# Gate products over 64 rows and one activation table in a hybrid decoder layer

## The chip, the core and the metric

The kernel runs on one core of one Trainium2 chip. The metric is the time of one execution on the device, in microseconds (us); every time given is that or a stretch of a profiled execution. The engines are TensorE (PE, with its weight loads as PEld), VectorE (DVE), ScalarE (ACT), GpSimd (POOL) and SyncE (SP, which only starts transfers here).

## What is computed

One layer over 1024 tokens and 16 meta tokens set ahead of them, model width 1024. After a norm, one projection gives queries, keys, values, and two streams of width 512, `x_rec` and `y_rec`. Attention runs in a sliding window of 128 with sinks. The other half of the heads is a gated linear recurrence, and this is where the change lies:

```
gate_r = einsum("btnc,ncd->btnd", xb, w_a) + b_a      # 8 blocks of 64 x 64
gate_i = einsum("btnc,ncd->btnd", xb, w_x) + b_x
r, i   = sigmoid(gate_r), sigmoid(gate_i)
log_a  = -8 * r * softplus(-lam)
a      = exp(log_a)
u      = sqrt(-expm1(2 * log_a)) * (i * x)
h[t]   = a[t] * h[t-1] + u[t]                          # along time
rec    = gelu(y_rec) * h
```

Here `x` is `x_rec` after a causal convolution over four steps. Attention and `rec` are joined, multiplied by `w_out` (1024 x 1024), normed and added. Then follow a norm and a feed-forward part of width 4096 with a squared ReLU, normed and added again. All inputs and outputs are float32.

## The kernel before

Every product is made in three parts: each operand is split into a high part, rounded for the matmul, and a low part, the rest. `split` (L93) does it with a cast (ACT unless told otherwise) and a subtraction on DVE; `mm3` (L122) multiplies high by high (L124), high by low (L125) and low by high (L126) into one PSUM bank. The feed-forward part, two thirds of the time, uses sums of blocks to save products; the change does not touch it but for one instruction.

The recurrence works with channels on the 128 partitions, four column groups `c` of 128 channels (two blocks of 64), and 1040 time steps along the free axis.

- `conv` (L606) leaves `xc[c]`. `gh` and `gl` (L691 and L692) hold the gate weights as 128 x 128 matrices, two 64 x 64 blocks on the diagonal and zeros besides; `graw` (L683) is cleared by POOL and filled by four transfers.
- `gates(c)` (L697) splits `xc[c]`, and for each of the two gates and each of three pieces of time (348, 348 and 344 steps) runs one `mm3` over 128 rows into a bank and evicts it with a sigmoid on ACT. Then DVE multiplies the input gate by `xc[c]` (L715).
- `decay(c)` (L719) makes `a` by an exponential and `tanh(-4 r softplus)` (a function in the exponential's table), both on ACT. Since `-expm1(2 log_a) = -tanh(log_a / 2) * (1 + a)^2`, the root of the tangent times `1 + a` is the factor that the reference calls `mult`.
- `recur(c)` (L725) takes the root on ACT (L727 by way of `lut`), then on DVE multiplies by `1 + a` (L728), by the gated input (L729), and scans along time (L730).
- `rec_out(c, half)` (L732) takes the GeLU of `y_rec`, multiplies by `h` on DVE (L736) and splits the product for the output matmul. `half` is rows 0 to 511 or 512 to 1023.
- `load_wo` and `split_wo` (L742 and L749) fetch and split the eight row blocks of `w_out`; `out_mm` (L787) multiplies a tile of 128 tokens by row blocks 0 to 3 (attention) and 4 to 7 (`rec`).

All activations that need a table go through `lut` (L81), which keeps them in program order on ACT. A change from one table to another puts a table load of its own on ACT (ACT_TABLE_LOAD in the profile, at L82).

The order on the engines is not the program's. A scheduler at build time runs through the program on an estimate of the durations, and gives every engine the ready instruction with the first place in the program; `deferred` (L73) sets a piece back by 1000 places, and `behind` (L105) puts an instruction after a given one without a wait. The order that comes out is fixed in the kernel; the chip adds only waits. So the projections of `y_rec` (`next_fill`, L658) are spread between attention and gates, and row blocks 0 to 3 of the output product of the first four token tiles fill PE while the recurrences are made. Tiles share buffers by tag: the split output weights 1 to 7 use tag "a", whose 16 buffers hold the normed input until the last projection is done.

At the very end, `finish_late` (L1235) needs a square root; L1322 takes one of a constant ahead of it, so that its table is there.

Of the kernel before, what the change touches and what calls it, by code (L numbers as in the profile page):

```python
# [37 lines left out]
def hybrid_layer(  # L38
# [42 lines left out]
    def lut(*args, **kwargs):  # L81
        ins = nc.scalar.activation(*args, **kwargs).ins  # L82
        if last_lut[0] is not None:
            tc.add_manual_dep(
                ins, last_lut[0],
                mybir.DependencyInfo(
                    mybir.DependencyClass.NoSync, mybir.DependencyReason.DATA
                ),
                reason="lut",
            )  # L90
        last_lut[0] = ins.name

    def split(hi, lo, src, eng=None):  # L93
        if eng is None:
# [381 lines left out]
    nc.vector.tensor_tensor(acc4, acc4, sv, op=ALU.mult)  # L476
    nc.vector.tensor_scalar(sv, lam, -1.0, 0.0, op0=ALU.mult, op1=ALU.max)
    nc.vector.scalar_tensor_tensor(sv, acc4, 2.0, sv, op0=ALU.mult, op1=ALU.add)
    m8sp = const.tile([P, NLRU], F32, name="m8sp")
    m4sp = const.tile([P, NLRU], F32, name="m4sp")  # L480
    nc.vector.tensor_scalar(m8sp, sv, -8.0, None, op0=ALU.mult)
    nc.vector.tensor_scalar(m4sp, sv, -4.0, None, op0=ALU.mult)


    def put_v(dst, src):
# [194 lines left out]
    attend(*prev)  # L680


    graw = slot("e", [P, 2, NLRU, P])  # L683
    behind(last_pow[0], nc.gpsimd.memset(graw, 0.0).ins)
    for i, w in enumerate((w_a, w_x)):
        for s in range(2):
            r = slice(HD * s, HD * s + HD)
            nc.sync.dma_start(
                graw[r, i, :, r], w[0, s::2].rearrange("n c d -> c n d")
            )  # L690
    gh = slot("e", [P, 2, NLRU, P], F32R)  # L691
    gl = slot("b", [P, 2, NLRU, P], F32R)  # L692
    split(gh, gl, graw)

    rg = [None] * NLRU

    def gates(c):  # L697
        ch, cl = pair("b", [P, TT])
        split(ch, cl, xc[c])
        rg[c] = []  # L700
        for i in range(2):
            t_ = slot("c", [P, TT])
            for t0, n in ((0, 348), (348, 348), (696, 344)):
                flip[0] += 1
                acc = bank(("s", "pt", "o")[flip[0] % 3])
                mm3(
                    acc[:, :n], (gh[:, i, c, :], gl[:, i, c, :]),
                    (ch[:, t0 : t0 + n], cl[:, t0 : t0 + n]), True, True,
                )
                lut(  # L710
                    t_[:, t0 : t0 + n], acc[:, :n], AF.Sigmoid,
                    bias=prm[:, c, 5 + i : 6 + i],
                )
            rg[c].append(t_)
        nc.vector.tensor_tensor(t_, t_, xc[c], op=ALU.mult)  # L715

    av = [None] * NLRU

    def decay(c):  # L719
        r = rg[c][0]  # L720
        av[c] = slot("b", [P, TT])
        lut(av[c], r, AF.Exp, scale=m8sp[:, c : c + 1])
        lut(r, r, AF.Tanh, scale=m4sp[:, c : c + 1])

    def recur(c):  # L725
        r, gi = rg[c]
        lut(r, r, AF.Sqrt, scale=-1.0)  # L727
        nc.vector.scalar_tensor_tensor(r, av[c], 1.0, r, op0=ALU.add, op1=ALU.mult)  # L728
        nc.vector.tensor_tensor(gi, gi, r, op=ALU.mult)  # L729
        nc.vector.tensor_tensor_scan(r, av[c], gi, 0.0, op0=ALU.mult, op1=ALU.add)  # L730

    def rec_out(c, half):  # L732
        o = 512 * half
# [18 lines left out]

    for c in range(NLRU):
        gates(c)
    next_fill()
    for cs in ((0, 1), (2, 3)):
        for c in cs:
            decay(c)
        for c in cs:
            recur(c)  # L760
    load_wo(0, "raw")
    load_wo(1, "raw")
    load_wo(2, "d")
# [529 lines left out]
    for n, (i, q) in enumerate(steps):  # L1293
# [25 lines left out]
            finish_half(q - 1)  # L1319
        if i == 6 and q == 4:  # L1320
            root = small.tile([P, 1], F32, name="root", tag="root")
            lut(root, half_pow, AF.Sqrt, scale=-1.0)  # L1322
    for j in range(4):
        parts = col_parts(6, j)
        for k in finish_late(j, accs[j], parts):
# [33 lines left out]
```

## Time and profile before

| | |
|---|---|
| median of 3 runs | 963.28 us (963.26 to 963.48) |
| profiled execution | 963.19 us, span 960.8 us |
| PE busy | 941.4 us, 4654 matmuls |
| DVE busy | 669.6 us, 945 instructions |
| ACT busy | 501.1 us, 822 instructions |
| POOL busy | 156.7 us, 202 instructions |
| mean granted PE clock | 0.998 of full |

The span is the time from the first to the last instruction of the profiled execution; its own time is a little longer. Busy shares overlap: the engines work side by side. A row of a timeline gives start, duration, engine, source line, operation, output and inputs, and in brackets the idle time before it and what ended it. A row of the windows view gives the stretch, its length, and the busy time of PE, PEld, DVE, ACT and POOL with instruction counts, then the granted clock, the DMA share and GB/s. Rows of groups give count, busy time, mean ns of one, and idle time before. Matmuls are pipelined, so their pace is read from the distance of their starts and not from their durations.

### The profile page before, as it was taken

To read this page: it belongs to the slowest core of one execution; us is meant where nothing else is said; L and a number is where in the kernel's file an instruction comes from. 1 tells how busy PE (TensorE), PEld (TensorE's weight loads), DVE (VectorE), ACT (ScalarE), POOL (GpSimd) and SP (SyncE) were. 2 spreads that over 40 slices of the span, in tenths; PEclk is the share of its full clock that TensorE was granted. 3 is DMA by queue.
4 is the path that set the end of the run, shared out by engine and by line. 5 is a ranking of instruction groups with operands and counts; after the bars stand their busy time and mean duration, and the time that the engine had idled before them with its cause. 6 is when DMAs were issued, how large, how long until landed. Compare 5 with 4: busy or idle time off the path is not lost.

```text
span 960.8 us, 12386 instructions
## 1 busy us (share of the span) xinstructions
PE 941.4 (98%) x4654; PEld 789.1 (82%) x4654; DVE 669.6 (70%) x945; ACT 501.1 (52%) x822; POOL 156.7 (16%) x202
## 2 busy tenths in 40 slices
PE   6999999999999999999999999999999999999997
PEld 6999998888788877888888888788888888888886
DVE  5579989756955796664655465568557776779884
ACT  7556676469634663443555556554433343435441
POOL 4015656600021100000111001100111100003020
PEclk9999999999999999999999999999999999999999
DMA  8111101111235457676546557623667765556422
GB/s 293 46 48 42 39 7 45 41 58 67 87 132 175 150 180 224 192 263 197 197 161 216 163 193 252 213 95 120 171 171 192 194 225 194 180 196 155 110 88 87
DMA packets 85626, 140.74 MB, mean 146 GB/s; under 512 B 5784, under 2 KB 48936, under 8 KB 85568
## 3 DMA queue, kind: packets, MB, share of 16 engines
q1 hardware_dynamic: 75104, 108.51, 34.5%
q0 software_dynamic: 9600, 29.36, 11.7%
q10 hardware_dynamic: 864, 2.10, 0.6%
q8 instruction: 36, 0.59, 0.3%
q14 instruction: 22, 0.18, 0.1%
HBM read 115.70 MB, written 23.07 MB: 144 GB/s over the span
## 4 chain that ended last, share of the span: by engine, by line
PE 88%; issue 5%; ACT 3%; DVE 2%; DMA 1%; POOL 1%; DVEq 0%; SPq 0%; POOLq 0%; ACTq 0%
PE ps_acc L124 11%; PE ps_acc L125 10%; PE ps_acc L126 10%; PE ps_s L126 6%; PE ps_s L125 6%; PE ps_s L124 6%; PE ps_pt L124 6%; PE ps_pt L125 6%; PE ps_pt L126 6%; PE ps_o L124 5%; PE ps_o L126 5%; PE ps_o L125 5%; PE ps_o L585 1%; ACT c L82 1%; PE ps_s L525 1%
## 5 line engine op out<-in xcount | busy, mean ns | idle before, releaser
L95 ACT CAST ws<-raw 128x1024 fp32r<-128x1024 f32 (+1 forms) x70 | 71.8, 1025 | 122.6 <-PE ps_o L125 45.1
L98 DVE TENSOR_TENSOR ws<-raw,ws 128x1024 fp32r<-128x1024 f32 (+1 forms) x71 | 86.3, 1215 | 47.9 <-ACT ws L95 47.8
L124 PE MATMUL ps_acc<-a,ws 128*128 128x256 f32 (+2 forms) x256 | 85.2, 333 | 0.0
L125 PE MATMUL ps_acc<-a,ws 128*128 128x256 f32 (+2 forms) x256 | 84.8, 331 | 0.0
L126 PE MATMUL ps_acc<-a,ws 128*128 128x256 f32 (+2 forms) x256 | 84.8, 332 | 0.0
L98 DVE TENSOR_TENSOR b<-b,b 128x1024 fp32r<-128x1024 f32 (+2 forms) x48 | 57.6, 1200 | 27.0 <-PE ps_o L125 17.4
L95 ACT CAST ws<-e 128x1024 fp32r<-128x1024 f32 x42 | 43.9, 1045 | 60.3 <-PE ps_o L125 26.7
L98 DVE TENSOR_TENSOR ws<-e,ws 128x1024 fp32r<-128x1024 f32 x42 | 51.3, 1222 | 23.0 <-ACT ws L95 23.0
L95 ACT CAST b<-b 128x1024 fp32r<-128x1024 f32 (+2 forms) x48 | 49.5, 1030 | 34.2 <-DVE b L862 33.4
L575 POOL TENSOR_SCALAR_AFFINE_SELECT c<-c 128x512 fp32r<-128x512 f32 x64 | 55.7, 893 | 27.3 <-ACT c L95 15.4
L169 POOL TENSOR_TENSOR rs<-ms,half_pow 128x1 f32<-128x1 f32 (+1 forms) x29 | 21.0, 730 | 211.0 <-DVE ms L165 209.6
L126 PEld LDWEIGHTS ps_acc<-a,ws 128*128 128x128 f32 x256 | 48.2, 188 | 4.9
L124 PEld LDWEIGHTS ps_acc<-a,ws 128*128 128x128 f32 x256 | 48.2, 188 | 4.2
L125 PEld LDWEIGHTS ps_acc<-a,ws 128*128 128x128 f32 x256 | 48.1, 188 | 4.2
L124 PE MATMUL ps_acc<-ws,b 128*128 128x512 f32 (+1 forms) x120 | 46.3, 386 | 0.0
L125 PE MATMUL ps_acc<-ws,b 128*128 128x512 f32 (+1 forms) x120 | 46.0, 384 | 0.0
L126 PE MATMUL ps_acc<-ws,b 128*128 128x512 f32 (+1 forms) x120 | 46.0, 384 | 0.0
L125 PE MATMUL ps_pt<-ws,b 128*128 128x512 f32 x112 | 44.2, 395 | 0.6 <-DVE ws L98 0.6
L126 PE MATMUL ps_pt<-ws,b 128*128 128x512 f32 x112 | 43.9, 392 | 0.0
L124 PE MATMUL ps_pt<-ws,b 128*128 128x512 f32 x112 | 43.9, 394 | 0.0
L124 PE MATMUL ps_s<-ws,b 128*128 128x512 f32 x110 | 43.3, 395 | 0.0
L126 PE MATMUL ps_s<-ws,b 128*128 128x512 f32 x110 | 43.2, 393 | 0.0
(393 smaller groups left out, 2713.4 us busy)
## 6 DMA issues: line engine op xcount, KB each, us to landing
raw<-in_w_ff_dram SPq DMA_DIRECT2D x58, 512.0 KB, 4.3
e<-in_w_ff_dram SPq DMA_DIRECT2D x42, 512.0 KB, 3.9
raw<-in_w_in_dram SPq DMA_DIRECT2D x12, 512.0 KB, 4.9
d<-in_w_ff_dram SPq DMA_DIRECT2D x12, 512.0 KB, 3.8
s_dram<-d POOLq DMA_DIRECT2D x12, 512.0 KB, 3.9
e<-in_w_ff_dram POOLq DMA_DIRECT2D x10, 512.0 KB, 5.4
raw<-in_w_ff_dram POOLq DMA_DIRECT2D x10, 512.0 KB, 5.6
c<-in_x_dram SPq DMA_DIRECT2D x8, 512.0 KB, 8.1
```

The source lines that it names most:

```text
L82: ins = nc.scalar.activation(*args, **kwargs).ins
L95: nc.scalar.copy(hi, src)
L98: low = nc.vector.tensor_tensor(lo, src, f32(hi), op=ALU.subtract).ins
L124: nc.tensor.matmul(dst, lh, rh, start=start, stop=False, skip_group_check=True)
L125: nc.tensor.matmul(dst, lh, rl, start=False, stop=False, skip_group_check=True)
L126: last_mm[0] = nc.tensor.matmul(dst, ll, rh, start=False, stop=stop, skip_group_check=True).ins.name
L169: last_pow[0] = nc.gpsimd.tensor_tensor(rs[:n], ms[:n], half_pow[:n], op=ALU.pow).ins.name
L525: nc.tensor.matmul(dst, q[h][:, c], hi, start=True, stop=False, skip_group_check=True,)
L575: nc.gpsimd.affine_select(out=m[:, :, side, :], in_=f32(m)[:, :, 1, :], pattern=[[0, 4], [-sign, P]], compare_op=op, fill=0.0, base=0, cha ...
L585: nc.tensor.matmul(po[:, :, oc : oc + n], v, m[:, :, pc : pc + n], start=first and k == 0, stop=last and k == 1, skip_group_check=True,)
```

## The change

The gate weights are no longer 128 x 128 matrices with zeros. For each block of 64 input channels, the weights of both gates lie side by side, 64 rows by 128 columns: `gw` is 128 x 4 x 2 x 64. The rows of the upper block hold the input gate first and the recurrence gate second, those of the lower block the other way round. `gates(c)` multiplies the two blocks by matmuls over 64 rows, alternately, into two banks. Each bank then holds both gates of one block of 64 channels, one gate on each half of the partitions. `gbias` holds the biases in that layout, halved.

The sigmoid becomes `(1 + tanh(g/2)) / 2`: the eviction is a tangent with scale 0.5. Two half-partition copies (to `v`) and two half-partition products bring the gates to their channels; the factors one half go into the constants `m4sp` and `m2sp` and the scale of the root. `decay(c - 1)` follows `gates(c)`, `decay(3)` the last filling projection, and the four `recur` come after that, so that all roots stand together. The memset of `graw` is gone. The root of a constant near the end is put behind the last split.

```diff
@@ lut
         last_lut[0] = ins.name
+        return ins
@@ constants
-    m8sp = const.tile([P, NLRU], F32, name="m8sp")
     m4sp = const.tile([P, NLRU], F32, name="m4sp")
-    nc.vector.tensor_scalar(m8sp, sv, -8.0, None, op0=ALU.mult)
+    m2sp = const.tile([P, NLRU], F32, name="m2sp")
     nc.vector.tensor_scalar(m4sp, sv, -4.0, None, op0=ALU.mult)
+    nc.vector.tensor_scalar(m2sp, sv, -2.0, None, op0=ALU.mult)
@@ gate weights
-    graw = slot("e", [P, 2, NLRU, P])
-    behind(last_pow[0], nc.gpsimd.memset(graw, 0.0).ins)
-    for i, w in enumerate((w_a, w_x)):
-        for s in range(2):
-            r = slice(HD * s, HD * s + HD)
+    graw = slot("e", [P, NLRU, 2, HD])
+    for s in range(2):
+        r = HALF[s]
+        for i, w in enumerate((w_x, w_a)):
             nc.sync.dma_start(
-                graw[r, i, :, r], w[0, s::2].rearrange("n c d -> c n d")
-            )
-    gh = slot("e", [P, 2, NLRU, P], F32R)
-    gl = slot("b", [P, 2, NLRU, P], F32R)
-    split(gh, gl, graw)
+                graw[r, :, i ^ s, :], w[0, s::2].rearrange("n c d -> c n d")
+            )
+    gw = [slot("e", [P, NLRU, 2, HD], F32R), slot("b", [P, NLRU, 2, HD], F32R)]
+    split(*gw, graw)
+    gbias = const.tile([P, 2, NLRU], F32, name="gbias")
+    for s in range(2):
+        for i in range(2):
+            nc.vector.tensor_scalar(
+                gbias[HALF[i ^ s], s, :], prm[HALF[s], :, 6 - i], 0.5, None,
+                op0=ALU.mult,
+            )
@@ gates
-        ch, cl = pair("b", [P, TT])
-        split(ch, cl, xc[c])
-        rg[c] = []
-        for i in range(2):
-            t_ = slot("c", [P, TT])
-            for t0, n in ((0, 348), (348, 348), (696, 344)):
+        halves_x = pair("b", [P, TT])
+        split(*halves_x, xc[c])
+        te, to = slot("b", [P, TT]), slot("c", [P, TT])
+        for t0, n in ((0, 348), (348, 348), (696, 344)):
+            accs = []
+            for s in range(2):
                 flip[0] += 1
-                acc = bank(("s", "pt", "o")[flip[0] % 3])
-                mm3(
-                    acc[:, :n], (gh[:, i, c, :], gl[:, i, c, :]),
-                    (ch[:, t0 : t0 + n], cl[:, t0 : t0 + n]), True, True,
+                accs.append(bank(("s", "pt", "o")[flip[0] % 3]))
+            for k, (a, b) in enumerate(((0, 0), (0, 1), (1, 0))):
+                for s in range(2):
+                    nc.tensor.matmul(
+                        accs[s][:, :n], gw[a][HALF[s], c], halves_x[b][HALF[s], t0 : t0 + n],
+                        start=k == 0, stop=k == 2, skip_group_check=True,
+                    )
+            for s, t_ in enumerate((te, to)):
+                lut(
+                    t_[:, t0 : t0 + n], accs[s][:, :n], AF.Tanh, scale=0.5,
+                    bias=gbias[:, s, c : c + 1],
                 )
-                lut(
-                    t_[:, t0 : t0 + n], acc[:, :n], AF.Sigmoid,
-                    bias=prm[:, c, 5 + i : 6 + i],
-                )
-            rg[c].append(t_)
-        nc.vector.tensor_tensor(t_, t_, xc[c], op=ALU.mult)
-
-    av = [None] * NLRU
+        v = slot("c", [P, TT])
+        lo, hi = HALF
+        nc.vector.tensor_copy(v[hi], to[lo])
+        nc.vector.scalar_tensor_tensor(
+            to[lo], te[lo], 1.0, xc[c][lo], op0=ALU.add, op1=ALU.mult
+        )
+        nc.vector.tensor_copy(v[lo], te[hi])
+        nc.vector.scalar_tensor_tensor(
+            to[hi], to[hi], 1.0, xc[c][hi], op0=ALU.add, op1=ALU.mult
+        )
+        rg[c] = v, to, te
@@ decay
-        r = rg[c][0]
-        av[c] = slot("b", [P, TT])
-        lut(av[c], r, AF.Exp, scale=m8sp[:, c : c + 1])
-        lut(r, r, AF.Tanh, scale=m4sp[:, c : c + 1])
+        v, _, te = rg[c]
+        lut(te, v, AF.Exp, scale=m4sp[:, c : c + 1], bias=m4sp[:, c : c + 1])
+        lut(v, v, AF.Tanh, scale=m2sp[:, c : c + 1], bias=m2sp[:, c : c + 1])
@@ recur
-        r, gi = rg[c]
-        lut(r, r, AF.Sqrt, scale=-1.0)
-        nc.vector.scalar_tensor_tensor(r, av[c], 1.0, r, op0=ALU.add, op1=ALU.mult)
+        r, gi, a = rg[c]
+        lut(r, r, AF.Sqrt, scale=-0.25)
+        nc.vector.scalar_tensor_tensor(r, a, 1.0, r, op0=ALU.add, op1=ALU.mult)
         nc.vector.tensor_tensor(gi, gi, r, op=ALU.mult)
-        nc.vector.tensor_tensor_scan(r, av[c], gi, 0.0, op0=ALU.mult, op1=ALU.add)
+        nc.vector.tensor_tensor_scan(r, a, gi, 0.0, op0=ALU.mult, op1=ALU.add)
@@ order
     for c in range(NLRU):
         gates(c)
+        if c:
+            decay(c - 1)
     next_fill()
-    for cs in ((0, 1), (2, 3)):
-        for c in cs:
-            decay(c)
-        for c in cs:
-            recur(c)
+    decay(3)
+    for c in range(NLRU):
+        recur(c)
@@ before the end
-            lut(root, half_pow, AF.Sqrt, scale=-1.0)
+            behind(w_low[0], lut(root, half_pow, AF.Sqrt, scale=-1.0))
```

## The prediction, on record before the change was built

> **What bounds the kernel now.** I read the page first: engine shares and the chain of work that ended last.
>
> ```profile
> span 960.8 us, 12386 instructions
> ...
> PE 941.4 (98%) x4654; PEld 789.1 (82%) x4654; DVE 669.6 (70%) x945; ACT 501.1 (52%) x822; POOL 156.7 (16%) x202
> ...
> PE 88%; issue 5%; ACT 3%; DVE 2%; DMA 1%; POOL 1%; DVEq 0%; SPq 0%; POOLq 0%; ACTq 0%
> ```
>
> The matmul engine is occupied for 98% of the span and makes up 88% of the chain, so a microsecond counts only if matmul time goes away or one of its few gaps closes. The profiled execution took 963.19 us, 2.4 us around a span of 960.8; the median of the three runs is 963.28, 0.09 above it. What the measurement can tell from no change is 0.2%, about 1.9 us.
>
> The edit sits in the gates and what follows them, so the next view is busy time by stretch: gates, the last projection, the output product of the first four row tiles, and two later stretches.
>
> ```profile
> 199.80:219.00 19.20, 19.20 (x107) 17.76 (x106) 6.04 (x6) 12.51 (x26) 0.00 (x0) 1.00 0.17 55
> 219.00:231.30 12.30, 12.30 (x55) 9.99 (x54) 5.57 (x7) 12.15 (x12) 0.00 (x0) 1.00 0.01 1
> 231.30:268.00 36.70, 35.55 (x153) 28.26 (x152) 35.05 (x35) 24.59 (x33) 0.00 (x0) 1.00 0.32 110
> 268.00:340.00 72.00, 72.00 (x347) 59.36 (x346) 46.95 (x71) 36.76 (x90) 11.95 (x24) 1.00 0.45 149
> 340.00:565.00 225.00, 224.32 (x969) 181.13 (x968) 138.18 (x174) 112.70 (x145) 17.57 (x29) 1.00 0.61 198
> ```
>
> After the length of a stretch come PE, PEld, DVE, ACT and POOL busy. PE is full everywhere, even in the gates, where ACT is busy 12.51 of 19.20 and DVE 6.04. The third stretch differs: PE idles 36.70 - 35.55 = 1.15 us and DVE works 35.05 of 36.70. From 268 on PE is full again and DVE at 47 of 72. So what PE wins before 268 should reach the end, and only DVE between 227 and 268 can take it back. The waits of PE between 198 and 270:
>
> ```profile
> PE ps_pt L124 <- ACT a L95: 0.6, 1, 0.6
> PE ps_pt L125 <- DVE ws L98: 0.6, 1, 0.6
> ```
>
> The first is the high half of an output weight, queued on ACT behind the GeLUs; the second is the low half of the first output weight, queued on DVE among the recurrences.
>
> **The change, part by part.**
>
> *Gate products.* Now one column group has two gates x three pieces x three products = 18 matmuls, all over 128 rows, half of them zeros. After it has three pieces x three products x two halves = 18 again, over 64 rows each, all still 348 or 344 columns wide. The count stays at 72. The third group now runs unbroken:
>
> ```profile
> 210.78 0.32 PE L124 MATMUL ps_s<-b,e 128*128 128x348 f32 x1
> ...
> 213.47 0.32 PE L126 MATMUL ps_o<-b,b 128*128 128x344 f32 x1
> 213.63 0.39 PE L124 MATMUL ps_acc<-a,ws 128*128 128x512 f32 x1
> ```
>
> 18 matmuls from 210.78 to 213.63 are 0.158 us each, 72 are 11.4 us. Anything is saved only if the matmuls of the two row halves run side by side; no row of this trace shows 64-row matmuls, so I bound it. Upper end of the cost: no overlap, 11.4 us, nothing saved. Lower end: a pair in the time of one, 36 x 0.158 = 5.7, saving 5.7. Between them stands the weight load, since each matmul keeps its own load of 128 columns:
>
> ```profile
> 60.58 0.28 PE L529 MATMUL ps_s<-km,b 128*128 128x128 f32 x1
> 60.69 0.27 PE L525 MATMUL ps_s<-b,b 128*128 128x128 f32 x1
> 60.80 0.27 PE L529 MATMUL ps_s<-b,b 128*128 128x128 f32 x1
> ```
>
> ```profile
> 60.52 0.19 PEld L529 LDWEIGHTS ps_s<-km,b 128*128 128x128 f32 x1
> ...
> 60.85 0.19 PEld L525 LDWEIGHTS ps_s<-b,b 128*128 128x128 f32 x1
> ```
>
> In the scores, matmuls of only 128 columns still start 0.11 us apart, and so do their loads (0.33 us for three steps). If loads stay one after another, 72 x 0.11 = 7.9 us, saving 3.5. I take this, the nearest row, and keep 0 and 5.7 for the range. The Trainium skill ("TensorE: Matmul & The Clock Gate", Part 3) has matmuls of distinct row groups run together, with a span of one matmul plus about 4 ns per tile; by that a pair costs 0.162 us and 72 save 5.5 us. No row here shows it; it is rival 1.
>
> *Switching the array.* The only matmuls on few rows are the parameter transposes:
>
> ```profile
> 53.38 0.38 PE L286 MATMUL ps_s<-ident,d 128*128 128x128 f32 x2
> 53.69 0.41 PE L439 MATMUL ps_o<-ident,d 8*128 8x8 f32 x4
> 54.03 0.76 PE L497 MATMUL ps_pt<-ident,c 128*128 128x128 f32 x5
> ```
>
> ```profile
> 53.69 0.32 PEld L439 LDWEIGHTS ps_o<-ident,d 8*128 8x128 f32 x4 [0.17 <-issue]
> ```
>
> Their first load starts with the first matmul, not ahead of it, after 0.17 us of load idle. With 0.11 us per full-size transpose the pair at 53.38 should have handed over at 53.60, so about 0.1 us is lost on the way in; I take as much on the way out. The gates come in some five blocks between projection matmuls, ten switches, 1.0 us. If they are cut up by piece (12 blocks, 24 switches at 0.17) it is 4.1, and 0 at best. The Trainium skill ("TensorEngine Tiling (Array Packing)", Key Properties) says that a change of tiling mode drains the array, which speaks against interleaving; the late load at 53.69 agrees with it.
>
> PE: -3.5 + 1.0 = **-2.5 us**.
>
> *ACT.* Rows from 198 to 250:
>
> ```profile
> L82 ACT ACT_TABLE_LOAD x7 | 9.0, 1283 | 0.1
> L82 ACT ACTIVATE c<-c,m4sp 128x1040 f32<-128x1040 f32 x4 | 4.7, 1162 | 0.1
> L82 ACT ACTIVATE b<-c,m8sp 128x1040 f32<-128x1040 f32 x4 | 4.6, 1158 | 0.0
> ...
> L82 ACT ACTIVATE c<-ps_s,prm 128x348 f32<-128x348 f32 x8 | 4.4, 554 | 6.5 <-PE ps_s L126 6.5
> ...
> L82 ACT ACTIVATE c<-c 128x1040 f32<-128x1040 f32 x4 | 4.1, 1065 | 0.0
> ```
>
> ```profile
> 201.26 0.55 ACT L82 ACTIVATE c<-ps_s,prm 128x348 f32<-128x348 f32 x1 [1.20 <-PE ps_s L126]
> ...
> 206.56 0.55 ACT L82 ACTIVATE c<-ps_s,prm 128x348 f32<-128x348 f32 x1 [1.58 <-PE ps_s L126]
> 207.03 0.55 ACT L82 ACTIVATE c<-ps_pt,prm 128x348 f32<-128x348 f32 x1
> ...
> 246.03 1.28 ACT L82 ACT_TABLE_LOAD   x1
> ```
>
> Seven table loads: sigmoid, exponential, square root, exponential, square root, GeLU, and square root again at 246.03 for the final norm. The tangent and exponential rows already share a table. The first, second, fourth and fifth go (one square root load stays), and the one at 246.03 moves to the last FFN steps, where 1.28 us fits into ACT's slack (52% busy over the span). That frees 5 x 1.28 = 6.4 us here; the 24 gate activations, 8 decays and 4 roots keep number and width. The 6.5 us that ACT now waits for gate products can hold three of the four decays. First root, from the first activation at 201.3: 24 x 0.47 + 8 x 1.16 + one split's cast (about 1.0) = 21.6, some 1 us of gaps left, load 1.28, root 1.07: 226.2, against 227.6 now. The ACT-caused PE wait goes: **-0.6 us**. The DVE-caused one I leave in place.
>
> *DVE.*
>
> ```profile
> 222.22 0.69 DVE L640 COPY d<-ps_acc 128x512 f32<-128x512 f32 x1 [1.62 <-PE ps_acc L126]
> 227.66 1.24 DVE L728 SCALAR_TENSOR_TENSOR c<-b,c 128x1040 f32<-128x1040 f32 x1 [4.75 <-ACT c L82]
> 228.82 0.69 DVE L97 CAST ws<-raw 128x1024 fp32r<-128x1024 f32 x1
> ...
> 264.45 1.90 DVE L98 TENSOR_TENSOR b<-d,b 128x512 fp32r<-128x512 f32 x3
> ```
>
> ```profile
> L730 DVE TENSOR_TENSOR_SCAN c<-b,c 128x1040 f32<-128x1040 f32 x4 | 9.3, 2322 | 0.0
> L729 DVE TENSOR_TENSOR c<-c,c 128x1040 f32<-128x1040 f32 x4 | 5.0, 1242 | 0.0
> L728 DVE SCALAR_TENSOR_TENSOR c<-b,c 128x1040 f32<-128x1040 f32 x4 | 4.9, 1235 | 4.8 <-ACT c L82 4.8
> ```
>
> Added per group: two half-partition copies and two half-partition products for the one product of L715 (1.24 us). Width, not partitions, should set their time: 2 x 0.69 (the L97 row) + 2 x 1.24 = 3.9, so +2.6, in all +10.5 us. It lies in 203 to 223, where DVE idles 13.16 of the first stretch's 19.20: free. Without that cover only the last group's copies (2.6 us) would delay its decay. Four bias scalings on 64x4 are noise. From 227.66 to 266.35 DVE runs without a gap, 38.7 us, and PE takes up the last low half about 1 us later:
>
> ```profile
> 237.83 0.40 PE L125 MATMUL ps_pt<-a,b 128*128 128x512 f32 x1
> ...
> 267.40 0.63 PE L126 MATMUL ps_pt<-a,b 128*128 128x512 f32 x2
> ```
>
> (The row at 237.83 is PE's first product with the second output weight's low half.) With the first root 1.4 us earlier and the same order, DVE ends at 265.0. PE may then be ahead by 1.4 + 1.05 = 2.45 us before DVE holds it. PE wants 2.5 + 0.6 = 3.1. What is late next is DVE's low halves. I count 2.6: a little of DVE's work for rows 512 on can slip behind.
>
> *Smaller parts.* The memset of L684 on POOL goes and the gate weights halve in width (a cast and a subtraction, about 0.5 us each); both lie in the attention tail under projection matmuls, 0. The four weight DMAs on SP keep number and bytes, and the output-weight loads behind them their slots. No wait is added but the ordering of the final root, behind a DVE split already issued.
>
> Sum: 963.19 - 2.6 = 960.6; on the median 960.7. **Forecast 960.6 us.**
>
> **Rivals.**
>
> 1. *Full overlap.* Pairs take the time of one: PE -5.7 + 1.0 - 0.6 = -5.3, and since the four scans come in one run DVE can leave the splits for rows 512 on to the end, so it doesn't hold PE. 957.9. For: the halves use different rows and different banks. Against: loads at 0.11 us steps. The skill's span rule, named above, belongs here.
>
> 2. *No overlap.* The pair runs in series: 0 + 1.0 - 0.6 = +0.4, 963.6. Then the change does not do what its pairing is for, and it is no change within 0.2%. For: every full-array pair in the trace runs in series.
>
> 3. *DVE puts the scans before the weight splits.* All four roots will end within some 3.2 us, so 4 x (1.24 + 1.24 + 2.32) = 19.2 us of recurrences are ready at once and stand ahead of the output weights' low halves in program order. Before the change fewer pieces precede them, because the roots come two by two. PE used the second weight's low half 6.5 us after the projection's end (237.83 against 231.3); with the projection 2.5 us earlier that is 235.3. DVE has it at 226.2 + 4.8k + 3.1, with k recurrences ahead and 0.69 + 2 x 1.2 for the splits. From k = 2 it decides: 238.9, 3.6 us late. With three ahead it is 8.4 us late: 960.6 + 8.4 = 969.0, slower. For: DVE is the full engine there, 35.05 of 36.70. Against: the weight cast at 228.82 stands right behind the first recurrence's first piece, so dependent pieces leave room for splits, and PE can do two of three products without low halves.
>
> **How the numbers follow.** Forecast 0.37, rival 1 0.30, rival 2 0.15, rival 3 0.18. The limit for faster is 961.4, for slower 965.2. Of the forecast a quarter falls within 0.2% (switches or DVE eat another microsecond), of rival 1 a twentieth, of rival 2 most; slower holds rival 3 and a little of rival 2. So faster 0.56, within 0.2% 0.24, slower 0.20. The range 957.0 to 966.5 takes in rival 1, rival 2, and rival 3 with two recurrences ahead; three or more lie above it, and below it full overlap without switches and both waits closed.
>
> **What the profile will show.** Pairing: gate matmuls 64*128 starting 0.08 (rival 1), 0.11 (forecast) or 0.16 us apart (rival 2). Switching: gaps at the edges of gate blocks. ACT: three table loads between 198 and 250, first root near 226. DVE: busy without a gap to about 265, copies near 0.7 us. Rival 3: PE waits on DVE L98 of the output weights between 230 and 250. I am wrong if PE idles more than 2 us there, or if gains before 268 don't arrive at the end.

## The result and the profile after

The changed kernel takes 965.93 us (median of 17 runs, 962.5 to 970.64) beside 962.37 us (median of 17 runs, 961.13 to 965.31) of the kernel before on the same chip. The ratio is 1.003 with a 95% interval of 1.0019 to 1.0041: it is slower by 0.3%, where a gain was forecast. The time lies inside the predicted range, the sign is wrong. The changed kernel's time goes with the clock that PE was granted: the ten executions with a mean granted clock of 0.996 or more have a median of 964.5 us, the seven below it 967.0.

The page of the changed kernel, whose profiled execution took 966.45 us:

```profile
span 964.8 us, 12400 instructions
...
PE 943.9 (98%) x4654; PEld 786.8 (82%) x4654; DVE 680.2 (71%) x961; ACT 495.5 (51%) x818; POOL 155.7 (16%) x201
...
PE 83%; DVE 6%; issue 5%; DMA 3%; ACT 2%; POOL 1%; SPq 0%; DVEq 0%; POOLq 0%
```

As many matmuls as before, but DVE, with 2% of the chain that ended last before, now holds 6% of it. Next the same stretches as in the prediction (gates, last projection, first output products), columns as there, and PE's only wait between 198 and 270:

```profile
199.80:219.00 19.20, 19.20 (x103) 13.49 (x102) 11.94 (x12) 11.01 (x18) 0.00 (x0) 1.00 0.09 28
219.00:231.30 12.30, 12.30 (x59) 9.05 (x58) 10.88 (x13) 10.28 (x17) 0.00 (x0) 1.00 0.26 87
231.30:268.00 36.70, 33.38 (x133) 26.39 (x132) 34.50 (x33) 24.04 (x31) 0.00 (x0) 0.91 0.23 72
```

```profile
PE ps_pt L127 <- DVE b L99: 3.3, 1, 3.3
```

The counts behind PE are the ones to read. In these three stretches PE begins 103 + 59 + 133 = 295 matmuls; before it was 107 + 55 + 153 = 315. Twenty fewer at 0.23 us are 4.6 us. Most are missing in the third stretch, where PE idles 3.3 us and the mean granted clock is 0.91.

**The pairs overlap fully.** Timeline of PE, the first block of gate products (now L714; the products of `mm3` are L125 to L127):

```profile
199.93 0.39 PE L125 MATMUL ps_acc<-a,ws 128*128 128x512 f32 x1
200.24 0.42 PE L714 MATMUL ps_s<-b,e 64*128 64x348 f32 x1
200.25 0.42 PE L714 MATMUL ps_pt<-b,e 64*128 64x348 f32 x1
200.51 0.32 PE L714 MATMUL ps_o<-b,e 64*128 64x348 f32 x1
200.51 0.32 PE L714 MATMUL ps_s<-b,e 64*128 64x348 f32 x1
...
201.62 0.32 PE L714 MATMUL ps_o<-b,b 64*128 64x344 f32 x1
201.87 0.50 PE L126 MATMUL ps_acc<-a,ws 128*128 128x512 f32 x1
202.21 0.39 PE L127 MATMUL ps_acc<-a,ws 128*128 128x512 f32 x1
```

Both halves start together, and the eight pairs from 200.51 to 201.62 are 1.11 / 7 = 0.159 us apart: a pair costs what one matmul cost before (0.158). The edges cost too. From the full-size product at 199.93 it is 0.31 us to the first pair (0.23 is usual), 0.27 to the second (0.159), at the end 0.25 to the next full-size product (0.159), and 0.34 to the one behind it (0.23). The excess is 0.08 + 0.11 + 0.09 + 0.11 = 0.39 us for one round trip. The second group is worse, since single 64-row products stand, each without its partner, between full-size ones:

```profile
206.37 0.39 PE L127 MATMUL ps_acc<-a,ws 128*128 128x512 f32 x1
206.69 0.42 PE L714 MATMUL ps_s<-b,e 64*128 64x348 f32 x1
207.04 0.50 PE L125 MATMUL ps_acc<-a,ws 128*128 128x512 f32 x1
207.47 0.42 PE L714 MATMUL ps_pt<-b,e 64*128 64x348 f32 x1
207.82 0.49 PE L126 MATMUL ps_acc<-a,ws 128*128 128x512 f32 x1
```

One product of each kind takes 207.47 - 206.69 = 0.78 us where 0.39 would do: 0.39 us again. Three such trips stand ahead of each of the last three groups' blocks. The 15 products that are left of such a group then make seven pairs, and the last one runs alone. So 12 of the 72 products have no partner, and 30 pairs form in place of 36.

**The gates are stretched.** Timeline of ACT: the first tangent of each of the four groups, the cast behind it, and the start of the roots.

```profile
201.34 0.55 ACT L82 ACTIVATE b<-ps_s,gbias 128x348 f32<-128x348 f32 x1 [1.77 <-PE ps_pt L714]
201.79 1.05 ACT L96 CAST b<-d 128x1040 fp32r<-128x1040 f32 x1
...
209.64 0.55 ACT L82 ACTIVATE b<-ps_s,gbias 128x348 f32<-128x348 f32 x1 [4.59 <-PE ps_pt L714]
210.09 1.05 ACT L96 CAST b<-d 128x1040 fp32r<-128x1040 f32 x1
...
217.82 0.55 ACT L82 ACTIVATE b<-ps_s,gbias 128x348 f32<-128x348 f32 x1 [2.03 <-PE ps_pt L714]
...
225.95 0.55 ACT L82 ACTIVATE b<-ps_s,gbias 128x348 f32<-128x348 f32 x1 [1.99 <-PE ps_pt L714]
...
236.13 1.28 ACT L82 ACT_TABLE_LOAD   x1
237.43 3.96 ACT L82 ACTIVATE c<-c 128x1040 f32<-128x1040 f32 x4
```

The groups are 8.2 us apart (before, 201.26 to 206.56: 5.3). The cast that the next group's products need starts 0.45 us behind the first tangent of this group, each time. So the roots start at 237.43.

**DVE and PE behind it.** Timeline of DVE: the first piece of the recurrences, the first product with a GeLU (L751, both halves of the rows), that product's low half, and DVE's last low halves. Then PE's timeline where it runs dry.

```profile
238.53 2.39 DVE L743 SCALAR_TENSOR_TENSOR c<-b,c 128x1040 f32<-128x1040 f32 x2 [2.20 <-ACT c L82]
...
253.32 1.29 DVE L751 TENSOR_TENSOR d<-d,c 128x512 f32<-128x512 f32 x2
...
261.31 0.67 DVE L99 TENSOR_TENSOR b<-d,b 128x512 fp32r<-128x512 f32 x1
...
268.98 1.89 DVE L99 TENSOR_TENSOR b<-d,b 128x512 fp32r<-128x512 f32 x3
```

```profile
258.32 0.40 PE L126 MATMUL ps_s<-a,b 128*128 128x512 f32 x1
262.03 0.80 PE L127 MATMUL ps_pt<-a,b 128*128 128x512 f32 x1 [3.32 <-DVE b L99]
262.62 0.63 PE L125 MATMUL ps_pt<-a,b 128*128 128x512 f32 x1
...
267.32 0.55 PE L127 MATMUL ps_acc<-a,b 128*128 128x512 f32 x1
267.70 0.39 PE L125 MATMUL ps_acc<-a,b 128*128 128x512 f32 x1
```

The recurrences begin 10.9 us later than before (227.66). The first low half comes 9.0 us later than in the kernel before:

```profile
252.33 0.69 DVE L98 TENSOR_TENSOR b<-d,b 128x512 fp32r<-128x512 f32 x1
```

PE waits 3.3 us for the first low half and then runs with starts 0.43 us apart instead of 0.23: 13 matmuls from 262.03 to 267.70 take 5.7 us where 3.0 would do.

The sum from these rows: 30 pairs, each saving 0.158, -4.7; 13 round trips (four blocks, nine singles) x 0.39 = +5.1; the wait +3.3; the half clock +2.7; the two waits of before, which are gone, -1.2. That is +5.2. Counted in order of start, PE's 1300th matmul comes at 197.85 where before it came at 197.05, the 1800th at 311.90 where it came at 306.12: the stretch cost 5.0 us. So the gate products by themselves take PE 0.4 us more than before, not less.

The two profiled executions differ by less, 966.45 - 963.19 = 3.26, and not by the gates alone. In this one PE also ran at half clock ahead of them, in the attention:

```profile
155.00:158.40 3.40, 1.70 (x12) 1.33 (x11) 3.31 (x14) 2.84 (x10) 1.27 (x1) 1.00 0.53 154
158.42:161.83 3.41, 3.41 (x19) 3.41 (x18) 3.31 (x12) 2.40 (x9) 0.67 (x1) 0.50 0.02 5
```

That cost 1.5 us: the 1050th matmul comes 0.7 us earlier than before, the 1100th 0.8 later. e1, e6 and e10 below run the same instructions there at full clock, so it belongs to this execution and not to the order of its instructions. Behind 306 PE makes up 1.9 us, 0.9 of it between 600 and 640 (39.04 busy against 38.14), and its first 1000 matmuls lie 0.7 us nearer to the start of the span. That gives 5.0 + 1.5 - 1.9 - 0.7 = 3.9, and the spans differ by 964.8 - 960.8 = 4.0.

### The profile page after: what moved, and what is told of

It reads as the page before. It is cut to its first block, busy times and chain, and to the rows that moved or that the text cites. A ratio compares the mean times of both kernels' runs of the same rounds, so it can differ in the third digit from the quotient of the medians.

```text
span 964.8 us, 12400 instructions
## 1 busy us (share of the span) xinstructions
PE 943.9 (98%) x4654; PEld 786.8 (82%) x4654; DVE 680.2 (71%) x961; ACT 495.5 (51%) x818; POOL 155.7 (16%) x201
## 4 chain that ended last, share of the span: by engine, by line
PE 83%; DVE 6%; issue 5%; DMA 3%; ACT 2%; POOL 1%; SPq 0%; DVEq 0%; POOLq 0%
PE ps_acc L127 10%; PE ps_acc L126 10%; PE ps_acc L125 10%; PE ps_s L127 6%; PE ps_pt L127 5%; PE ps_s L126 5%; PE ps_pt L126 5%; PE ps_s L125 5%; PE ps_pt L125 5%; PE ps_o L127 4%; PE ps_o L126 4%; PE ps_o L125 4%; PE ps_o L586 1%; DVE a L877 1%; DVE ws L99 1%
## 5 line engine op out<-in xcount | busy, mean ns | idle before, releaser
L125 PE MATMUL ps_acc<-a,ws 128*128 128x256 f32 (+2 forms) x256 | 86.4, 338 | 0.0
L126 PE MATMUL ps_acc<-a,ws 128*128 128x256 f32 (+2 forms) x256 | 85.9, 336 | 0.0
L127 PE MATMUL ps_acc<-a,ws 128*128 128x256 f32 (+2 forms) x256 | 85.8, 336 | 0.0
L125 PEld LDWEIGHTS ps_acc<-a,ws 128*128 128x128 f32 x256 | 49.1, 192 | 5.1 <-issue 0.9
L127 PEld LDWEIGHTS ps_acc<-a,ws 128*128 128x128 f32 x256 | 48.9, 191 | 5.2 <-issue 0.5
L126 PEld LDWEIGHTS ps_acc<-a,ws 128*128 128x128 f32 x256 | 48.9, 191 | 5.0 <-issue 0.9
L125 PE MATMUL ps_acc<-ws,b 128*128 128x512 f32 (+1 forms) x120 | 46.2, 385 | 0.0
L127 PE MATMUL ps_acc<-ws,b 128*128 128x512 f32 (+1 forms) x120 | 46.0, 384 | 0.0
L127 PE MATMUL ps_pt<-ws,b 128*128 128x512 f32 x112 | 44.0, 393 | 0.0
L125 PE MATMUL ps_pt<-ws,b 128*128 128x512 f32 x112 | 43.9, 392 | 0.0
L125 PE MATMUL ps_s<-ws,b 128*128 128x512 f32 x110 | 43.3, 394 | 0.0
```

Source lines behind the costliest of these rows:

```text
L125: nc.tensor.matmul(dst, lh, rh, start=start, stop=False, skip_group_check=True)
L126: nc.tensor.matmul(dst, lh, rl, start=False, stop=False, skip_group_check=True)
L127: last_mm[0] = nc.tensor.matmul(dst, ll, rh, start=False, stop=stop, skip_group_check=True).ins.name
```

## The experiments

Two questions had to be told apart: what stretches the gates, and whether that or something behind it costs the time. In the first four expectations the letters of the theories are about the gates; from e5 on, theory A is that PE has become quicker than the chain from the roots over DVE to the low halves, and loses its lead there. Ratios are against runs of the kernel before beside them, with 95% intervals.

### e1: the casts of the gates' input ahead of the gates

In the changed kernel `te` takes a buffer of tag "b" in `gates(c)`, ahead of the pair that `gates(c + 1)` asks for. Here the pairs of three groups are asked for first.

```diff
+    def split_x(c):
+        hx[c] = pair("b", [P, TT])
+        split(*hx[c], xc[c])
+    for c in range(3):
+        split_x(c)
     for c in range(NLRU):
         gates(c)
+        if c == 0:
+            split_x(3)
```

> The changed kernel, but the splits of the first three column groups are written ahead of the gates, so that their buffers of tag b are given out before the gate tiles te of the same tag; nothing is left out. Theory A (the gates were stretched because te stands in the line for b buffers ahead of the next group's split): the four groups' first gate activations come 5.5 to 6.5 us apart instead of 8.2, the first root ends near 231 instead of 238.5, PE no longer waits 3.3 us for a low half near 260 and keeps its full clock there: 957 to 960 us, faster than before the change by 2 to 5. Theory B (the decays between the groups hold up the next activations on ACT): spacing stays above 7.5 us, 963 to 966. Theory C (switching the array between 64-row and 128-row matmuls eats the overlap): 962 to 965, with PE waits gone but no gain over before.

Measured: 962.79 us, ratio 0.9993 (0.9982 to 1.0003). The groups start at 200.31, 207.15, 213.89 and 219.76, the roots at 232.75, and no single 64-row product is left between full-size ones. But PE's waits between 198 and 270 and its third stretch are:

```profile
PE ps_pt L127 <- DVE b L99: 3.3, 1, 3.3
PE ps_pt L125 <- ACT b L96: 1.0, 1, 1.0
```

```profile
231.30:268.00 36.70, 32.40 (x132) 25.51 (x131) 32.44 (x33) 19.36 (x27) 0.00 (x0) 0.95 0.25 77
```

So the late casts are what stretched the gates, and their price is about what the change lost (1.003 to 0.9993). That price lies in PE's own work: 36 pairs and four round trips are -5.7 + 1.6 = -4.1 here, where the changed kernel had +0.4. But the gain that PE then has is all given back: it idles 4.3 us and begins 132 matmuls where before it began 153. That the waits would go with the late casts was wrong.

### e2: late casts kept, all decays behind the gates

```diff
     for c in range(NLRU):
         gates(c)
-        if c:
-            decay(c - 1)
...
-    decay(3)
+    for c in range(NLRU):
+        decay(c)
```

> The changed kernel, with all four decays after the last gates instead of between them. Theory A: the splits still wait for buffers, so the groups stay 6 us or more apart, and the decays, 8 x 1.28 us, now come on top: first root no earlier than 237, 964 to 967 us. Theory B: the groups close up to 5 us, the first root comes by 233 and the time falls to 959 to 962.

Measured: 970.04 us, ratio 1.007 (1.0058 to 1.0082), above theory A's 964 to 967. Two rows of ACT:

```profile
200.08 0.55 ACT L82 ACTIVATE b<-ps_s,gbias 128x348 f32<-128x348 f32 x1 [1.77 <-PE ps_pt L714]
...
208.38 0.55 ACT L82 ACTIVATE b<-ps_s,gbias 128x348 f32<-128x348 f32 x1 [4.59 <-PE ps_pt L714]
```

Without any decay between them the groups are still 8.1 to 8.3 us apart; ACT idles where the decays stood (4.5 us ahead of the third group, 2.0 in the changed kernel). The decays don't stretch the gates; moved behind them they only make the roots later (241.7) and the time longer.

### e3: tangents and one group of roots, products over 128 rows

```diff
-                    t_[:, t0 : t0 + n], acc[:, :n], AF.Sigmoid,
-                    bias=prm[:, c, 5 + i : 6 + i],
+                    t_[:, t0 : t0 + n], acc[:, :n], AF.Tanh, scale=0.5,
+                    bias=hbias[:, c, i : i + 1],
...
     for c in range(NLRU):
         gates(c)
+        if c == 3:
+            for k in range(3):
+                decay(k)
```

The gate products and their weights are those of before, and so is the one DVE product but for a `+ 1`; three decays follow the last gates, and the little root near the end is ordered as in the change.

> The kernel before, with its 128-row gate products, but with tangents for sigmoids, decays after the gates, and all roots in one group. The split buffers are given out as before. Theory A: the table loads that go free ACT, the first root comes at 229 or earlier, and since PE has no less work the time is that of before less at most the 1.2 us of PE waits: 961 to 962.5. Rival 3 of the prediction (all scans ready at once push the weight splits back on DVE): PE waits between 230 and 250, 964 to 969.

Measured: 962.98 us, ratio 1.0 (0.999 to 1.0009). The groups are 4.9 to 5.3 us apart (201.04 to 216.17), the roots start at 230.96, and PE waits 0.7 us for the first low half. Five table loads fewer by themselves give nothing: the 0.6 us that PE waited for ACT before are gone, and 0.7 us for DVE stand in their place.

### e4: pairs with early casts, sigmoids and two groups of roots

e1 with the sigmoids, the constants and the order of decays and roots of before.

```diff
-                    t_[:, t0 : t0 + n], accs[s][:, :n], AF.Tanh, scale=0.5,
+                    t_[:, t0 : t0 + n], accs[s][:, :n], AF.Sigmoid,
...
-        if c:
-            decay(c - 1)
...
+    for cs in ((0, 1), (2, 3)):
+        for c in cs:
+            decay(c)
+        for c in cs:
+            recur(c)
```

> The changed kernel's 64-row pairs, with sigmoids, tables, decays and roots in the order of before, and the splits written ahead as in the first kernel here. Theory A: PE saves 5.7 us less some 1.5 of switching; ACT and DVE have the late chain of before, with 2.6 us more of DVE work per group under cover, so part is lost again to waits near 245: 959 to 961.5. Theory C: switching eats it, 962 to 964.

Measured: 964.2 us, ratio 1.0014 (1.0002 to 1.0025), slower than either theory's range. PE's wait:

```profile
PE ps_pt L125 <- ACT b L96: 5.1, 1, 5.1
```

Here too PE gets ahead and loses it: the last roots come at 244.38 and the GeLUs behind them at 246.77, so the first product's high half is 5.1 us late, and the clock between 250 and 260 is 0.66.

### e5: the second half of the rows held behind the first

e1 with this edit:

```diff
-        nc.vector.tensor_tensor(y, y, h[:, NMETA + o : NMETA + o + 512], op=ALU.mult)
+        ins = nc.vector.tensor_tensor(
+            y, y, h[:, NMETA + o : NMETA + o + 512], op=ALU.mult
+        ).ins
+        if half:
+            behind(low_0[0], ins)
...
-        split(ah[:, c % 2, :], al[:, c % 2, :], y)
+        low = split(ah[:, c % 2, :], al[:, c % 2, :], y)
+        if not half:
+            low_0[0] = low.name
```

> The changed kernel with early casts (e1, 962.8 us), and on DVE the four products for the second 512 tokens held behind the last low half of the first 512. That takes 4 x 0.6 us out of the row of DVE work for which TensorE waited in e1 (3.3 us for the first low half of the recurrence's output, and half a clock after it). Theory A (TensorE has become quicker than the chain roots, combine, scan, product, low half, and its lead is lost in that wait): the first low half 1 us earlier, the wait 2 to 2.5 us, the time 961 to 962.5. Theory B (the lead is lost for another reason, later in the kernel): 962.8 within 0.5, with the idle time showing up behind 268.

Measured: 961.49 us, ratio 0.9984 (0.9972 to 0.9997), an interval that overlaps e1's. The profiled execution is the quickest of the twelve, 959.57 us. In it PE waits 2.2 us for the first low half and 0.8 us for ACT, and the clock stays at 1.00, as theory A had it. In others the mean granted clock goes down to 0.995, so the half clock is not gone for good.

### e6: one channel group after the other on DVE

In `recur`, besides e5's edit (`a0`, `a1` and `a2` are the combine, the product and the scan):

```diff
+        for ins in (a0.ins, a1.ins, a2.ins):
+            if prev_r[0] is not None:
+                behind(prev_r[0], ins)
+            prev_r[0] = ins.name
```

> As e5, and DVE takes combine, product and scan of one channel block after the other in place of all combines first. The first low half is then due about 244 to 247 in place of 256.6, in front of the time (253.9) at which TensorE ran dry in e1. Theory A: no wait of TensorE over 1 us before 268, the clock stays at 1.00 there, and the pairs' gain arrives: 957 to 960. Theory B (what TensorE wins before 268 is given back at a later wait): 962 to 963.5 with the new wait behind 268.

Measured: 955.65 us (954.93 to 957.67, 4 runs), ratio 0.9925 (0.9907 to 0.9943): the fastest kernel here, 0.75% below the one before. The four executions all have a mean granted clock of 0.998 or more. Rows of DVE (the first piece, the first low half) and PE's third stretch:

```profile
234.05 1.24 DVE L748 SCALAR_TENSOR_TENSOR c<-b,c 128x1040 f32<-128x1040 f32 x1 [2.44 <-ACT c L82]
...
246.96 0.69 DVE L99 TENSOR_TENSOR b<-d,b 128x512 fp32r<-128x512 f32 x1
```

```profile
231.30:268.00 36.70, 36.70 (x160) 29.73 (x159) 33.20 (x34) 21.87 (x34) 0.16 (x1) 1.00 0.20 65
```

DVE starts no earlier than in e1 (233.85), but the first low half is there at 246.96 in place of 256.64. PE has no wait between 190 and 290, begins 160 matmuls where e1 began 132, and the time drops by 0.7%. The same DVE work in another order: theory B falls.

### e7: the same order on DVE in the kernel before

The kernel before with the diffs of e5 and e6, nothing else.

> The control: the kernel before the change with e6's order on DVE alone (128-row gate products, sigmoids, two groups of roots). Theory A: TensorE waited little there in the kernel before, so the order alone is worth 0 to 1 us: 962 to 963.3 beside a before of 963. Rival: the order itself is what pays, and this kernel is as fast as e6.

Measured: 963.41 us, ratio 0.9997 (0.9984 to 1.001). PE waits 1.5 us for ACT's cast of an output weight, where before it waited 0.6 for ACT and 0.6 for DVE. The order by itself gives nothing; with 128-row products, sigmoids and two groups of roots PE has no lead to lose there.

### e8: the two products of a pair in series

e1 with this edit:

```diff
-            for k, (a, b) in enumerate(((0, 0), (0, 1), (1, 0))):
-                for s in range(2):
+            for s in range(2):
+                for k, (a, b) in enumerate(((0, 0), (0, 1), (1, 0))):
```

> e1 with the two 64-row products of a bank pair issued one after the other (three products into one bank, then three into the other), so that they no longer run side by side. TensorE then needs about 36 x 0.157 = 5.7 us more in the gates. Theory A (TensorE's lead is lost in the wait for DVE): that wait and its half clock shrink by as much and the time stays near e1's, 962.5 to 964.5. Theory B (each microsecond of TensorE before 268 arrives at the end): 968 to 969.

Measured: 962.77 us, ratio 0.9998 (0.9986 to 1.001), as theory A had it, but the edit did not do what it was for. In this kernel's order three products into bank `o` stand ahead of the three into bank `s`, and PE's timeline shows:

```profile
206.28 0.32 PE L719 MATMUL ps_o<-b,e 64*128 64x348 f32 x1
206.30 0.31 PE L719 MATMUL ps_s<-b,e 64*128 64x348 f32 x1
206.44 0.32 PE L719 MATMUL ps_o<-b,b 64*128 64x348 f32 x1
206.46 0.31 PE L719 MATMUL ps_s<-b,b 64*128 64x348 f32 x1
```

They still run side by side. So this run says nothing on theory A or B; it says that the order within a block of pairs doesn't matter. It also corrects what was said of the kernel before, that the chip adds only waits to the order: here products start ahead of others that stand before them.

### e9: e3 with e6's order on DVE

e3 with the diffs of e5 and e6. The products are over 128 rows, so there are no pairs.

> e3 (128-row gate products of the kernel before, tangents and one group of roots; 962.98 us) with e6's order on DVE. Set beside e6 it gives what the pairs alone are worth where nothing waits. Theory A (TensorE's work arrives at the end once its wait for DVE is gone): e6's 955.7 and some 4.5 us more (36 pairs x 0.157 us saved less four changes of shape at 0.3), 959 to 961. Rival (the order on DVE pays for itself, whatever the products): 955 to 957, as e6.

Measured: 960.66 us, ratio 0.9973 (0.9961 to 0.9985). PE's third stretch:

```profile
231.30:268.00 36.70, 36.70 (x160) 29.75 (x159) 35.42 (x36) 21.22 (x34) 0.00 (x0) 1.00 0.23 73
```

Nothing waits here either, so the distance to e6 is what the pairs are worth when their gain arrives: 0.9973 - 0.9925 of 963 is 4.6 us, and the intervals don't touch. From the rows it would be 5.7 less four round trips at 0.39, 4.1. The tangents and the order on DVE together are worth 0.27% without any pairs, though neither gives anything alone (e3, e7).

### e10: the changed kernel with e6's order on DVE

The changed kernel with the diffs of e5 and e6; the casts stay late.

> The changed kernel as it is, with its late casts and its gate groups 8.2 us apart, and e6's order on DVE alone. Tells the two causes apart. Theory A: the first low half is due about 251 in place of 260 and TensorE, which ran dry at 258.7, does not wait for it; what is left is the single 64-row products set between 128-row ones (nine round trips at 0.39 us, 3.5 us): 958 to 960. Rival (the late gates are a cost by themselves that the order cannot hide): 962 to 966, with TensorE waiting for the last channel's low half instead.

Measured: 960.03 us, ratio 0.9969 (0.9954 to 0.9985).

```profile
231.30:268.00 36.70, 36.70 (x160) 29.79 (x159) 33.68 (x32) 21.87 (x29) 0.00 (x0) 1.00 0.23 72
```

With its late casts and roots at 236.00 the changed kernel still feeds PE, if the first channel's low half isn't put behind the other channels' scans. The late gates leave it 4.2 us behind e6 (0.9969 against 0.9925): nine round trips more at 0.39 us, 3.5, and six pairs fewer, 0.9, make 4.4. With late casts the pairs are worth nothing, and this kernel stands where e9 does without them (0.9973).

### e11: e4 with e6's order on DVE

e4 with the diffs of e5 and e6.

> e4 (pairs, sigmoids and two groups of roots; 964.2 us) with e6's order on DVE: what the tangents and the one group of roots are worth where the order is good. The second group's roots end at 246 in e4, so the third and fourth channels are late whatever DVE's order. Theory A: TensorE waits about 2 to 4 us there, for ACT's cast of the first product or for the later channels: 957 to 961. Rival (the sigmoid tables cost nothing, since ACT has idle time): 955.7, as e6.

Measured: 963.77 us, ratio 1.0008 (0.9993 to 1.0023), slower than either theory's number. PE's wait of 5.1 us for ACT is unchanged; ACT's rows show why:

```profile
247.83 0.63 ACT L82 ACTIVATE d<-d 128x512 f32<-128x512 f32 x1
...
252.11 1.28 ACT L82 ACT_TABLE_LOAD   x1
253.40 0.20 ACT L82 ACTIVATE root<-half_pow 128x1 f32<-128x1 f32 x1
253.51 1.03 ACT L96 CAST a<-d 128x1024 fp32r<-128x1024 f32 x1
254.44 0.61 ACT L96 CAST b<-d 128x512 fp32r<-128x512 f32 x1
```

The GeLUs wait for the second group of roots, and then all eight GeLUs, a table load, the little root of the last stage and a weight cast stand ahead of the cast that PE waits for. DVE's order can't help where ACT is late. So the pairs' gain does not arrive with the sigmoids, two groups of roots and the little root where they were before: by the ratios e6 is 8.0 us faster than e11. What each of the three is worth here is not separated; e12 takes back the little root alone.

### e12: e6 without the order of the last stage's root

```diff
-            behind(w_low[0], lut(root, half_pow, AF.Sqrt, scale=-1.0))
+            lut(root, half_pow, AF.Sqrt, scale=-1.0)
```

> e6 without the order that holds the little root of the last stage behind that stage's low half. The scheduler then puts that root and a table load of 1.28 us behind the GeLUs of 238 to 242 on ACT. Both theories: ACT has idle time behind 243, so 955.7 within 1; a wait of TensorE for ACT's cast near 244 to 246 would make it up to 1.5 us slower.

Measured: 957.32 us (955.2 to 960.82, 6 runs), ratio 0.9942 (0.992 to 0.9963), an interval that overlaps e6's. PE has no wait between 190 and 290. The three executions with a mean granted clock of 0.999 took 955.2 to 956.6 us, like e6; the three at 0.997 took longer, and the profiled one of these has its half clock at 161.3, ahead of the gates. Whether this order is worth anything is not settled.

The runs side by side, ratios to the kernel before:

| | order of DVE as scheduled | one channel group after the other, second half held |
|---|---|---|
| before | 1 | e7 0.9997 |
| changed | 1.003 | e10 0.9969 |
| changed, early casts | e1 0.9993 | e6 0.9925 |
| tangents alone | e3 1.0 | e9 0.9973 |
| pairs alone, early casts | e4 1.0014 | e11 1.0008 |

## Why the prediction was wrong

**The first step that failed is the one on ACT:** "First root, from the first activation at 201.3 ... 226.2", and with it "No wait is added". The first root ended near 238.5, 12.3 us later than that step said. e1 splits the error. Without the late casts the roots start at 232.75, so 237.43 - 232.75 = 4.7 us are the wait for buffers: the new tile `te` stands between the pairs of tag "b" in program order, and the next group's cast could only start when the first tangent had been written. I counted tiles' durations and not the order in which they ask for buffers. The rest, 7.6 us, is there in e1 as well. ACT still idles 6.6 us between its first tangent and the roots, 5.4 for gate products and 1.2 for a DMA, where the step had 1 us of gaps (+5.5). Three casts of output weights stand among the decays (+3.0), and a decay with a bias from a column takes 1.28 us in place of 1.16 (+0.8 for eight, overlaps counted). The tangents are a little quicker than assumed (-0.8), and e1 starts 1.0 us earlier. The table loads came out as the step counted them: of seven, four go and one moves, which leaves two between 198 and 250, for the roots and the GeLUs. The three that the prediction's list of signs names is a slip.

**"What PE wins before 268 should reach the end, and only DVE between 227 and 268 can take it back".** The place was right, and DVE took it back. What failed is the size that I gave it, "PE may then be ahead by 2.45 us" and "a little of DVE's work for rows 512 on can slip behind". I measured DVE by the end of its run; PE was held by the first low half. In the changed kernel the first product is made at 253.32 and its low half at 261.31, with a weight split, two scans and the second channel group's product between. e6 shows that this was order and not amount. PE had not become quicker either, its gate work had grown by 0.4 us; the low half had moved from 252.33 to 261.31. This second failed step decides the sign: e10 keeps the late casts and the late roots, changes only the order on DVE, and is at 0.9969.

**Pairs.** I took the weight loads in series, 7.9 us, saving 3.5; rival 1 had full overlap and 5.7. Measured: full overlap where a pair forms, but 30 pairs of 36, so 4.7. By the span rule of the Trainium skill ("TensorE: Matmul & The Clock Gate", Part 3) a pair would take an estimated 0.162 us, which agrees with the 0.159 measured here.

**Switching.** I had ten switches at 0.1 us, 1.0; the bound for cut-up blocks was 4.1. Measured: 0.39 us a round trip and 13 of them, 5.1. The late casts made nine of these. So PE's own work rose by 0.4 us, where the sum had -2.5; with the casts in time (e1, e6) it fell by 4.1.

**DVE's added work** was sized rightly (copies 0.70, products 1.24 us) and hidden, as said. The trace shows no cost of the smaller parts.

**The half clock** stood in no step. Behind the 3.3 us of idle time PE lost another 2.7 us to it in the changed kernel's profiled execution, and 1.5 us in the attention.

**Rivals.** Rival 2 is out. Rival 1 was right on what a pair takes; e6, where all pairs form and nothing waits, is at 955.65, below its 957.9. Rival 3 named the right kind of mechanism, four recurrences in one run ahead of splits that PE needs, at the wrong place: PE never waited for a weight's low half between 230 and 250, but for the low half of the recurrence's own output at 261. PE did not idle more than 2 us in that stretch, which was one sign of being wrong; the other, that gains before 268 do not arrive at the end, is what e1 shows. The range held the measured time because it was drawn wide enough for rival 3, which is not what happened: that was luck.

**Shown and argued.** That the late casts stretch the gates is shown (e1, e2), as are the loss to DVE's order (e6, e10), the worth of the pairs where nothing waits (e9 beside e6), and that neither the order nor the tangents alone give it before (e7, e3). What set off the half clock in each execution is not shown. That the casts wait for buffers in program order is inferred from the edit of e1 and the fixed 0.45 us behind the first tangent. Their place in the program alone does not explain it, since in the kernel before the casts stand at the same place and the groups are 5.3 us apart.

## What to carry to other kernels

When a change makes a full engine quicker, find the first result that it will wait for next, and date that result, not the end of the run of work that it stands in. A lead counts only if the chain beside it is ordered for it: here the same DVE work in another order turned a loss of 0.3% into a gain of 0.3%, and with casts in time into 0.75%. A new tile in a shared tag is a new wait for whoever asks for that tag next.

## What the runs showed of the hardware

- Two matmuls over 64 rows each into different banks start together, and so do their weight loads (two at 200.67 in the changed kernel's timeline of loads); pairs follow at 0.159 us with 348 columns. They needn't alternate in the program: in e8 a product ran beside one that stood three places behind it.
- A change between full-size and 64-row products and back costs 0.39 us, however few products stand between.
- PE fell to half clock around an idle time of 3.3 us (changed kernel: starts 0.43 us apart until 267.3; e1: 0.42 apart from 258.5 to 261.5, beginning about a microsecond after work had resumed). It also fell to it at 158.4 in the changed kernel, behind waits of 0.44 and 1.26 us, with PE busy for 1.70 of the 3.40 us before; and e5's waits of 0.8 and 2.2 us led to none (clock 1.00 in its profiled execution). So the length of a wait does not settle it. The Trainium skill ("TensorE: Matmul & The Clock Gate", Part 1) puts the half clock down to a free-running window of about 3.4 us. The stretches at half clock, 3.4 us (158.4 to 161.8) and 6.8 us (260.8 to 267.7), agree with that, and such a window would also let the time of one kernel vary; the changed kernel's runs range over 8.1 us.
- A decay with scale and bias from columns takes 1.28 us for 1040 columns on ACT, with scale alone 1.16 us.
